# One layer of a hybrid decoder: both output projections with pairs of column blocks and seven products in place of eight

## The chip, the cores and the metric

The kernel runs on one core of a Trainium2 chip. Its engines work from queues of their own: TensorE (PE, matmuls; its weight loads are listed as PEld), VectorE (DVE), ScalarE (ACT), GpSimd (POOL, which here issues DMAs) and SyncE (SP, which issues DMAs). The metric is the time of one execution in microseconds (us) on the device. The kernel before took 1468.19 to 1469.03 us in three runs, with a median of 1468.9 us.

## What is computed

One layer over 256 tokens with a model width of 2048, in float32. Cut to what matters here:

```python
def hybrid_mixer(h, w_in, ...):
    c_q, c_kv, k_r, q_s, k_s, v_s, gates = jnp.split(h @ w_in, offsets, axis=-1)
    ...
    o_a = mla_attention(...)                       # 256 x 2048
    o_b = swa_attention(q_s, k_s, v_s, swa_sinks, rel_table)
    g = jax.nn.sigmoid(gates).reshape(B, S, 2, D_MODEL)
    merged = g[:, :, 0] * (o_a @ w_o_mla) + g[:, :, 1] * (o_b @ w_o_swa)
    return merged @ w_out

def reference(x, ...):
    h = rms_norm(x, norm_mix_pre)
    y = hybrid_mixer(h, ...)
    x = x + rms_norm(y, norm_mix_post)
    h = rms_norm(x, norm_ffn_pre)
    return x + rms_norm(conv_ffn(h, ...), norm_ffn_post)
```

The two products that the change touches are `o_a @ w_o_mla`, called the latent branch's output projection below, and `merged @ w_out`, called the mixer's projection. Each multiplies 256 x 2048 activations by a 2048 x 2048 matrix.

## The kernel before

**How a product is made.** Every float32 product is three matmuls: both operands are split into a high part and a low part, and `mm3` (L175 to L177) adds high by high, high by low and low by high into one PSUM bank. Activations lie transposed in SBUF as sixteen k-rows of 128 x 256 (a high and a low tile each); the 256 tokens are two halves of 128, which are a matmul's stationary operand (128 x 128), and the weights are its moving operand, 512 columns at a time.

**A block.** `gemm` computes 512 columns of the result in eight chunks of two k-rows. For each chunk SP loads 512 KB of weights (`raw`, L131), ACT copies it to the high part (`whi`, L143), DVE subtracts to get the low part (`wlo`, L144), and PE makes 2 k-rows x 2 token halves x 3 = 12 matmuls. The tiles come from rings: RAW = 3 raw tiles and RING = 4 pairs of `whi` and `wlo`, and two "flex" tiles are added to the raw ring or to the other, as `flex[0]` says. So the loads and splits run a few chunks ahead of PE.

**A pair.** `pair_gemm` computes two blocks (1024 columns) in eight units of two k-rows, in the order of a string. A plain unit "p" is 24 matmuls with two SP loads and two splits of 1024 columns. A unit "s" makes seven products of 128 x 128 by 128 x 512 (21 matmuls) from sums of its operands in place of eight. For it `place()` names two tiles, POOL loads the two k-rows into them (L227 the even row, L228 the odd one), DVE makes four sums of 128 x 512 of the weights (L232 to L235, in the tiles of `sums()`), and four splits follow, of the odd row, half of the even row, and the two tiles of sums. `token_sums` (L278 to L284, then a split, L317 and L318) makes the sums of the activations for one unit. The last "s" ends with additions over four more PSUM banks q1, q5, q7, q6 (L255 to L261). The two token halves and two blocks need four banks c11 to c22, so a pair occupies all eight banks. Before the change the branch gates (c and q banks named `cg`, `qg`, order "psppspsp") and the down projection of the FFN (`cd`, `qd`; `cdb`, `qdb`) use it.

**The stretch that is changed.** The gates `ta` of the latent branch are the last work of the input's projection. POOL stores them (L904, `ta_d`). Then the latent branch's projection runs as four single blocks over `wo_a` on the activation tiles `AH` and `AL`; before each block `merge_loads` has POOL load `ta` and the other branch's result `yb` for its 512 columns (tiles `lta`, `lyb`), and after it DVE forms (1 + ta) x acc + yb in `lta` (L955 and L956). A chunk or two into the next block, `m_cols` transposes this on PE (`mT`, L935) and ACT and DVE split it into the slots `mt` (L320, L321), which are the activation of the mixer's projection. That one again runs as four blocks over `w_out` (`flex[0] = "w"` from its start); each is squared and summed on ACT (L972) and multiplied by the norm's gain `gpost` on DVE (L973) into `yg`. The last block feeds the residual sum, the transposes for the FFN (`x2T`), and then the FFN itself.

**What sets the order.** `at(t, f)` puts a function into the step that ends chunk t; `tick()` runs the functions due. A scheduler then sets each engine's order from that of the program: it keeps near it, but puts an instruction behind others whose operands and tiles come free earlier. `late_loads` spreads twelve SP loads over the first block: four of `gpost`, eight of `x` for the residual. Pool `px` holds the `whi` and `wlo` ring tiles and three spare pairs; pool `p6` holds `gpost` (tag "gp") and `yg` (tags "fa" and "fb", two of 128 x 1024 each).

## Time and profile before

| what | value |
|---|---|
| runs | 1468.19 to 1469.03 us, median 1468.9 |
| the profiled execution | 1470.05 us, of which its span is 1468.3 |
| PE busy | 1456.9 us, 7576 instructions |
| DVE busy, ACT busy | 1067.2 us, 830.5 us |
| gates end, latent branch's projection starts | about 553.5 us |
| mixer's projection | about 645 to 735 us |
| granted TensorE clock in these stretches | 1.00 |

The profile is that of one execution: its span is the time from the first to the last instruction, and 1.75 us of the 1470.05 lie outside it. Times in it are microseconds from the span's start. A matmul of 512 columns is listed with some 0.39 us from start to end, but matmuls are pipelined, so what each costs is the distance from one start to the next. In a row of instructions "out<-in" names the tiles, "xN" the count, and what stands in brackets is the idle time before it and what ended that.

### The profile page before, as it was taken

The page shows a single profiled execution, that of the slowest core. Times are in us where ns is not written, and L with a number is a line of the kernel's source. Part 1 is how long each engine was busy: PE and PEld are TensorE (multiplying, and loading weights), DVE is VectorE, ACT ScalarE, POOL GpSimd, SP SyncE. Part 2 cuts the span into 40 slices and gives each one's busy share as a digit, 9 for nine tenths or more (in the row PEclk, how much of TensorE's full clock was granted, in tenths as well). Part 3 has the DMA queues.
Part 4 walks back from the last instruction along what each step waited for, and adds up shares of the span by engine and source line. Part 5 has one row for each costly group of instructions (what it writes and reads, how often), then busy time and mean ns, then how long its engine had stood idle before and what let it go on. Part 6 is the DMA issues. An engine that isn't in the chain of part 4 may idle for free.

```text
span 1468.3 us, 20938 instructions
## 1 busy us (share of the span) xinstructions
PE 1456.9 (99%) x7576; PEld 1244.8 (85%) x7576; DVE 1067.2 (73%) x1881; ACT 830.5 (57%) x1372; POOL 64.9 (4%) x113
## 2 busy tenths in 40 slices
PE   9999999999999999999999999999999999999997
PEld 7888888888888888888888888888888888888886
DVE  7688896745667665555699976778776687677775
ACT  7588874543555554444566655555454565555453
POOL 0011110000000000000000000000000000000000
PEclk9999999999999999999999999999999999999999
DMA  8755376466655559756766666665656666667573
GB/s 297 211 164 167 108 259 192 162 212 200 191 156 160 164 163 334 226 184 212 225 205 185 188 193 193 187 187 187 218 174 213 198 187 189 187 197 233 163 237 129
DMA packets 149909, 287.60 MB, mean 196 GB/s; under 512 B 18428, under 2 KB 29597, under 8 KB 149677
## 3 DMA queue, kind: packets, MB, share of 16 engines
q1 hardware_dynamic: 141312, 256.80, 56.5%
q0 software_dynamic: 8400, 29.41, 6.4%
q8 instruction: 59, 0.97, 0.3%
q14 instruction: 46, 0.37, 0.1%
q10 hardware_dynamic: 92, 0.05, 0.0%
HBM read 277.79 MB, written 8.44 MB: 195 GB/s over the span
## 4 chain that ended last, share of the span: by engine, by line
PE 97%; DVE 2%; ACT 1%; issue 0%; DMA 0%; DVEq 0%; ACTq 0%
PE accg L175 13%; PE accg L177 13%; PE accg L176 13%; PE ub L1147 10%; PE ua L1147 10%; PE ua L1151 5%; PE ub L1151 5%; PE cd L177 2%; PE cd L175 2%; PE cd L176 2%; PE cdb L175 1%; PE cdb L177 1%; PE cdb L176 1%; PE mpo L875 1%; PE cg L176 1%; PE cg L177 1%
## 5 line engine op out<-in xcount | busy, mean ns | idle before, releaser
L144 DVE TENSOR_TENSOR wlo<-raw,whi 128x1024 fp32r<-128x1024 f32 (+2 forms) x476 | 576.3, 1214 | 282.5 <-ACT whi L143 275.2
L143 ACT CAST whi<-raw 128x1024 fp32r<-128x1024 f32 (+2 forms) x476 | 494.7, 1043 | 427.5 <-PE accg L177 172.3
L175 PE MATMUL accg<-whi,ahl 128*128 128x512 f32 (+1 forms) x480 | 187.9, 392 | 0.0
L177 PE MATMUL accg<-whi,ahl 128*128 128x512 f32 (+1 forms) x480 | 185.6, 387 | 0.0
L176 PE MATMUL accg<-wlo,ahl 128*128 128x512 f32 (+1 forms) x480 | 184.8, 385 | 0.0
L1147 PE MATMUL ua<-ahl,whi 128*128 128x512 f32 x640 | 154.6, 391 | 0.0
L1147 PE MATMUL ub<-ahl,whi 128*128 128x512 f32 x640 | 154.6, 391 | 0.0
L175 PE MATMUL accg<-whi,bhl 128*128 128x512 f32 x378 | 148.2, 392 | 0.0
L177 PE MATMUL accg<-whi,bhl 128*128 128x512 f32 x378 | 147.4, 390 | 0.0
L176 PE MATMUL accg<-wlo,bhl 128*128 128x512 f32 x378 | 147.3, 390 | 0.0
L1147 PEld LDWEIGHTS ub<-ahl,whi 128*128 128x128 f32 x640 | 117.5, 188 | 22.9 <-ACT cc L1045 0.2
L1147 PEld LDWEIGHTS ua<-ahl,whi 128*128 128x128 f32 x640 | 117.6, 188 | 22.7
L177 PEld LDWEIGHTS accg<-whi,ahl 128*128 128x128 f32 x480 | 90.1, 188 | 18.0
L176 PEld LDWEIGHTS accg<-wlo,ahl 128*128 128x128 f32 x480 | 90.3, 188 | 15.6
L175 PEld LDWEIGHTS accg<-whi,ahl 128*128 128x128 f32 x480 | 90.3, 188 | 15.5
L1151 PEld LDWEIGHTS ub<-ahl,wlo 128*128 128x128 f32 x640 | 82.2, 191 | 3.2
L1151 PEld LDWEIGHTS ua<-ahl,wlo 128*128 128x128 f32 x640 | 82.2, 191 | 3.1
L1151 PE MATMUL ua<-ahl,wlo 128*128 128x256 f32 x640 | 83.7, 283 | 0.0
L177 PEld LDWEIGHTS accg<-whi,bhl 128*128 128x128 f32 x378 | 71.0, 188 | 14.8
L176 PEld LDWEIGHTS accg<-wlo,bhl 128*128 128x128 f32 x378 | 71.0, 188 | 14.5
L1151 PE MATMUL ub<-ahl,wlo 128*128 128x256 f32 x640 | 83.2, 283 | 0.0
L175 PEld LDWEIGHTS accg<-whi,bhl 128*128 128x128 f32 x378 | 71.0, 188 | 14.3
(545 smaller groups left out, 2218.9 us busy)
## 6 DMA issues: line engine op xcount, KB each, us to landing
raw<-in_ffn_w_up_dram SPq DMA_DIRECT2D x176, 512.0 KB, 4.5
raw<-in_w_in_dram SPq DMA_DIRECT2D x105, 512.0 KB, 4.5
raw<-in_ffn_w_down_dram SPq DMA_DIRECT2D x68, 512.0 KB, 4.5
raw<-in_w_o_swa_dram SPq DMA_DIRECT2D x32, 512.0 KB, 4.4
raw<-in_w_o_mla_dram SPq DMA_DIRECT2D x32, 512.0 KB, 4.5
raw<-in_w_out_dram SPq DMA_DIRECT2D x32, 512.0 KB, 4.1
bias<-strip POOLq DMA_DIRECT2D x16, 256.0 KB, 4.4
raw<-in_mla_w_q_up_dram SPq DMA_DIRECT2D x32, 128.0 KB, 2.8
```

Of the source, the lines that this page charges most:

```text
L143: act.copy(hi[:, a:b], raw[:, a:b])
L144: vec.tensor_tensor(lo[:, a:b], raw[:, a:b], hi[:, a:b].bitcast(F32), op=ALU.subtract)
L175: pe.matmul(o, ah, bh, start=start, stop=False)
L176: pe.matmul(o, ah, bl, start=False, stop=False)
L177: pe.matmul(o, al, bh, start=False, stop=stop)
L875: pe.matmul(o, w(t), p_[:, c], start=n == 0, stop=n == 5)
L1147: pe.matmul(acc[i], hi[:, c], hn[p][:, j * 512:(j + 1) * 512], start=p + j == 0, stop=stop)
L1151: pe.matmul(acc[i][:, 0:256], lo[:, c], hn[p][:, j * 512:j * 512 + 256], start=False, stop=False)
```

## The change

The latent branch's projection becomes a single block 0, a pair of blocks 1 and 2 in the order "pppsppsp" (two units of seven), and a single block 3. The mixer's projection becomes a pair of blocks 0 and 1 in the order "ppspspsp" (three units of seven), and single blocks 2 and 3. Single blocks 0 and 3 of the first and 2 of the second write to the PSUM banks "s", since the pairs take "acc" first.

The sums of tokens for the seven products are made ahead: `a_sums` (tiles `as0`, `as1`) in the course of block 0, `m_sums` (`ms0`, `ms1`) during the first pair, and `ms2` in block 3. The tiles that these and the POOL loads need are all spare ones taken in turn: the spare `whi` and `wlo` tiles of `px` hold `as`, `ms`, the second unit's `ar2hi` and `ar2lo` of the first pair, `lyb2` and the odd units' `mr` of the second pair; the "gp" tile holds `ar1`, the temporary `mtmp` and `mr2` before `gpost`; "fa" and "fb" hold the temporaries `at`, the sums `ta` of the weights and `ud` before `yg`. Therefore `gpost` is now loaded by POOL, two chunks after the second unit of the mixer's pair, in place of SP during block 0. `lta` has four buffers in place of three. The two flex tiles stay with the raw ring until the last block of the mixer's projection. The pool after `es4` opens behind the pair.

```diff
     es6, p6 = open_pool("p6")
-    gpost = sb(p6, [P, D], "gpost", tag="gp")
+    gpost = []
     def late_loads(i):
         if i < 4:
-            nc.sync.dma_start(gpost[:, i * 512:(i + 1) * 512], g_mix_post[i * 512:(i + 1) * 512].partition_broadcast(P))
+            if i == 0:
+                gpost.append(sb(p6, [P, D], "gpost", tag="gp"))
+            pool.dma_start(gpost[0][:, i * 512:(i + 1) * 512], g_mix_post[i * 512:(i + 1) * 512].partition_broadcast(P))
         else:
             t, j = divmod(i - 4, 4)
             nc.sync.dma_start(x2[t][j], x[t * P:(t + 1) * P, j * 512:(j + 1) * 512])
                 pe.transpose(pt[:, i * 256 + t * P:i * 256 + (t + 1) * P], ld[t][0][:, c:c + P], ident)
         split_to(mth[p][:, :], mtl[p][:, :], pt, 0.5)
-    def merge_loads(j):
+    def merge_loads(j, kinds="ab"):
         ld = []
         for t in range(NT):
-            a = sb(p4, [P, 512], f"lta{j}_{t}", tag="lta", bufs=3)
-            b = sb(p4, [P, 512], f"lyb{j}_{t}", tag="lyb", bufs=2)
-            pool.dma_start(a, ta_d[j, t])
-            pool.dma_start(b, yb_d[j, t])
-            ld.append((a, b))
+            both = []
+            for kind, tag, src, bufs in (("a", "lta", ta_d, 4), ("b", "lyb", yb_d, 2)):
+                if kind in kinds:
+                    both.append(sb(p4, [P, 512], f"{tag}{j}_{t}", tag=tag, bufs=bufs))
+                    pool.dma_start(both[-1], src[j, t])
+            ld.append(both)
         return ld
-    for i in range(12):
+    as_ = {}
+    def a_sums(u):
+        st = sb(px, [P, 1024], f"as{u}", F32R, tag="w" + ("hi", "lo")[u % 2])
+        tmp = sb(p6, [P, 1024], f"at{u}", tag="f" + "ab"[u % 2], bufs=2)
+        as_[u] = token_sums(at_[u].bitcast(F32), tmp[:, 0:512], tmp[:, 512:1024], st[:, 0:512], st[:, 512:1024])
+    def merged(a, b, acc):
+        vec.scalar_tensor_tensor(a, a, 1.0, acc, op0=ALU.add, op1=ALU.mult)
+        vec.tensor_tensor(a, a, b, op=ALU.add)
+    a_done = [0]
+    def a_place():
+        a_done[0] += 1
+        i = a_done[0]
+        if i % 2:
+            both = sb(p6, [P, D], f"ar{i}", tag="gp")
+            return both[:, 0:1024], both[:, 1024:2048]
+        return [sb(px, [P, 1024], f"ar{i}{n}", tag="w" + n) for n in ("hi", "lo")]
+    ud_a = []
+    def f_pair(name):
+        return [sb(p6, [P, 1024], f"{name}{n}{cnt[0]}", tag="f" + n, bufs=2) for n in "ab"]
+    def ud_place():
+        ud_a[:] = [x_[:, j * 512:(j + 1) * 512] for x_ in f_pair("ud") for j in range(2)]
+        return ud_a
+    def single(j, lead=3):
+        ld = merge_loads(j)
+        acc, _ = gemm(AH, AL, wo_a, 0, KT, 512 * j, 512, ps=(pss, "s"))
+        for t in range(NT):
+            merged(*ld[t], acc[t])
+        for p in range(2):
+            at(now[0] + lead + p, lambda p=2 * j + p, ld=ld: m_cols(p, ld))
+    def a_pair():
+        lds = [merge_loads(1), merge_loads(2, "a")]
+        both = sb(px, [P, 1024], "lyb2", tag="whi")
+        for t in range(NT):
+            lds[1][t].append(both[:, t * 512:(t + 1) * 512])
+            pool.dma_start(lds[1][t][1], yb_d[2, t])
+        c = pair_gemm("a", wo_a, 0, 512, A_ORDER, lambda k, t: (AH(k)[:, t * P:(t + 1) * P], AL(k)[:, t * P:(t + 1) * P]),
+                      lambda u: as_[u], 0, ud_place, a_place, lambda: f_pair("ta"))
+        def pair_evac(i):
+            t, j = divmod(i, 2)
+            vec.tensor_tensor(ud_a[i], ud_a[i], c[i], op=ALU.add)
+            merged(*lds[j][t], ud_a[i])
+        for n_, i in enumerate((0, 2, 1, 3)):
+            at(now[0] + n_, lambda i=i: pair_evac(i))
+        for p in range(2, 6):
+            at(now[0] + 2 + p, lambda p=p: m_cols(p, lds[p // 2 - 1]))
+    for u in range(A_ORDER.count("s")):
+        at(now[0] + 1 + 3 * u, lambda u=u: a_sums(u))
+    for i in range(4, 12):
         at(now[0] + 10 + 2 * i, lambda i=i: late_loads(i))
-    for j in range(4):
-        ld = merge_loads(j)
-        acc, _ = gemm(AH, AL, wo_a, 0, KT, 512 * j, 512)
-        for t in range(NT):
-            a, b = ld[t]
-            vec.scalar_tensor_tensor(a, a, 1.0, acc[t], op0=ALU.add, op1=ALU.mult)
-            vec.tensor_tensor(a, a, b, op=ALU.add)
-        for p in range(2):
-            at(now[0] + (3 if j == 3 else 1) + p, lambda p=2 * j + p, ld=ld: m_cols(p, ld))
+    ms = {}
+    def m_sums(u):
+        st = sb(px, [P, 1024], f"ms{u}", F32R, tag="w" + ("hi", "lo")[u % 2])
+        tmp = sb(p6, [P, D], f"mtmp{u}", tag="gp")
+        ms[u] = token_sums(mt[u].bitcast(F32), tmp[:, 0:512], tmp[:, 512:1024], st[:, 0:512], st[:, 512:1024])
+    single(0)
+    for u, t in ((0, 9), (1, 12)):
+        at(now[0] + t, lambda u=u: m_sums(u))
+    a_pair()
     yg_all = [[sb(p6, [P, 1024], f"yg_{t}_{j}", tag="f" + "ab"[t], bufs=2) for j in range(2)] for t in range(NT)]
     yg = [[yg_all[t][j // 2][:, (j % 2) * 512:(j % 2 + 1) * 512] for j in range(4)] for t in range(NT)]
+    at(now[0] + 6, lambda: m_sums(2))
+    single(3, 2)
     blocks = [(0, 512), (512, 512), (1024, 512), (1536, 256), (1792, 256)]
     NB = len(blocks)
     W_BLOCKS = [(512 * j, 512) for j in range(4)]
...
-        vec.tensor_tensor(yg[t][j][:, o:o + n], acc[t][:, :n], gpost[:, c0:c0 + n], op=ALU.mult)
+        vec.tensor_tensor(yg[t][j][:, o:o + n], acc[t][:, :n], gpost[0][:, c0:c0 + n], op=ALU.mult)
...
-    flex[0] = "w"
-    turn.update(raw=0, w=0)
-    for b in range(4):
+    w_done = [0]
+    def w_place():
+        w_done[0] += 1
+        i = w_done[0]
+        if i % 2:
+            return [sb(px, [P, 1024], f"mr{i}{n}", tag="w" + n) for n in ("hi", "lo")]
+        both = sb(p6, [P, D], f"mr{i}", tag="gp")
+        at(now[0] + 2, *(lambda k=k: late_loads(k) for k in range(4)))
+        return both[:, 0:1024], both[:, 1024:2048]
+    def w_pair():
+        d = [yg[t][j] for t in range(NT) for j in range(2)]
+        c = pair_gemm("w", w_out, 0, 0, W_ORDER, lambda k, t: (MH_(k)[:, t * P:(t + 1) * P], ML_(k)[:, t * P:(t + 1) * P]),
+                      lambda u: ms[u], 0, d, w_place, lambda: [yg_all[t][1] for t in range(NT)])
+        def pair_evac(i):
+            t, j = divmod(i, 2)
+            vec.tensor_tensor(d[i], d[i], c[i], op=ALU.add)
+            act.activation(jk(f"yj{j}_{t}"), d[i], AF.Square, accum_out=ssy[t][:, j:j + 1])
+            vec.tensor_tensor(d[i], d[i], gpost[0][:, j * 512:(j + 1) * 512], op=ALU.mult)
+        for i in range(4):
+            at(now[0] + i, lambda i=i: pair_evac(i))
+    w_pair()
+    es4.close()
+    es8, p8 = open_pool("p8")
+    for b in range(2, 4):
         c0, n = W_BLOCKS[b]
         last = b == 3
-        acc, todo = gemm(MH_, ML_, w_out, 0, KT, c0, n, split=0 if last else None, extra={i: (px,) for i in range(EXTRA)} if last else None)
-        if b == 0:
+        if last:
+            flex[0] = "w"
+            turn.update(raw=0, w=0)
+        acc, todo = gemm(MH_, ML_, w_out, 0, KT, c0, n, split=0 if last else None, extra={i: (px,) for i in range(EXTRA)} if last else None,
+                         ps=None if last else (pss, "s"))
+        if last:
             drain()
-            es4.close()
-            es8, p8 = open_pool("p8")
-        if last:
             y_evac(acc, b, 0)
             resid(0)
             finish_tile(acc[1], todo)
...
+A_ORDER = "pppsppsp"
+W_ORDER = "ppspspsp"
```

The program has 15 matmul rows fewer on PE (7386 rows before, 7371 now). The instructions move as follows at three places.

**DVE during block 0 of the latent branch's projection.** `wlo` are the splits of the block's chunks, four of which precede these rows; `at` is the temporary of the token sums, `bhl` the activation's slots. Before:

```order
L144 TENSOR_TENSOR wlo_5912<-raw_5909,whi_5911 128x1024
L144 TENSOR_TENSOR wlo_5930<-raw_5927,whi_5929 128x1024
L144 TENSOR_TENSOR wlo_5948<-raw_5945,whi_5947 128x1024
L144 TENSOR_TENSOR wlo_5966<-raw_5963,whi_5965 128x1024
L144 TENSOR_TENSOR wlo_5984<-raw_5981,whi_5983 128x1024
L144 TENSOR_TENSOR wlo_6002<-raw_5999,whi_6001 128x1024
```

Now:

```order
L144 TENSOR_TENSOR wlo_5938<-raw_5935,whi_5937 128x1024
L278 TENSOR_TENSOR at_5909<-bhl_4096 128x512
L144 TENSOR_TENSOR wlo_5956<-raw_5953,whi_5955 128x1024
L281 TENSOR_TENSOR at_5909<-at_5909 128x128
L282 TENSOR_TENSOR at_5909<-at_5909 128x128
L283 TENSOR_TENSOR at_5909<-at_5909 128x128
L278 TENSOR_TENSOR at_5972<-bhl_4097 128x512
L284 TENSOR_TENSOR at_5909<-at_5909 128x128
L281 TENSOR_TENSOR at_5972<-at_5972 128x128
L282 TENSOR_TENSOR at_5972<-at_5972 128x128
L283 TENSOR_TENSOR at_5972<-at_5972 128x128
L144 TENSOR_TENSOR wlo_5983<-raw_5980,whi_5982 128x1024
```

The sums of two units stand between the splits of the chunks, up to eight rows of them between one split and the next.

**POOL from the stores of the last gates on.** Each row is a DMA that POOL issues; in brackets are the counters that it waits for (DMASW the queue's own earlier DMAs, then PE, ACT and DVE). `ta_0_5832` and `ta_1_5835` are the last gates. Before:

```order
L904 DMA ta_d<-ta_0_5832 128x512 [waits DMASW2_49,Activation_49]
L904 DMA ta_d<-ta_1_5835 128x512 [waits DMASW3_49,Activation_49]
L944 DMA lyb_0_6022<-yb_d 128x512 [waits DMASW6_49,DMASW4_49,DVE_49]
L944 DMA lyb_1_6026<-yb_d 128x512 [waits DMASW5_49,DMASW0_49,DVE_49]
L943 DMA lta_1_6025<-ta_d 128x512 [waits PE_49]
L943 DMA lta_0_6196<-ta_d 128x512 [waits DMASW7_49,PE_49]
L944 DMA lyb_0_6197<-yb_d 128x512 [waits DMASW4_49,DVE_49]
```

Now:

```order
L904 DMA ta_d<-ta_0_5832 128x512 [waits DMASW3_49,Activation_49]
L904 DMA ta_d<-ta_1_5835 128x512 [waits DMASW4_49,Activation_49]
L227 DMA ar_6179<-in_w_o_mla_dram 128x1024 [waits DMASW5_49,DMASW4_49,DMASW3_49]
L228 DMA ar_6179<-in_w_o_mla_dram 128x1024 [waits DMASW6_49]
L994 DMA lyb_6050<-yb_d 128x512 [waits DMASW7_49]
L994 DMA lyb_6050<-yb_d 128x512 [waits DMASW0_49]
L228 DMA ar2lo<-in_w_o_mla_dram 128x1024 [waits DMASW1_49]
L947 DMA lyb_0_6040<-yb_d 128x512 [waits DMASW2_49,DVE_49]
L947 DMA lyb_1_6044<-yb_d 128x512 [waits DVE_49]
L947 DMA lta_0_6046<-ta_d 128x512 [waits PE_49]
L947 DMA lta_1_6048<-ta_d 128x512 [waits DMASW5_49,PE_49]
L227 DMA ar2hi<-in_w_o_mla_dram 128x1024 [waits DMASW6_49,PE_49,Activation_49]
```

Four loads of weight rows of 512 KB (`ar` twice, `ar2lo`, `ar2hi`) stand in this queue now, among the loads for the merge; `ar2hi`, the last, waits for PE and ACT as well.

**DVE at the start of the mixer's projection.** `lta` are the merged columns of the latent branch's last block, `mT` the transposes, `ahl` their slots. Before:

```order
L955 SCALAR_TENSOR_TENSOR lta_0_6372<-lta_0_6372,accg_0_6380 128x512
L955 SCALAR_TENSOR_TENSOR lta_1_6376<-lta_1_6376,accg_1_6381 128x512
L956 TENSOR_TENSOR lta_0_6372<-lta_0_6372,lyb_0_6373 128x512
L956 TENSOR_TENSOR lta_1_6376<-lta_1_6376,lyb_1_6377 128x512
L144 TENSOR_TENSOR wlo_6624<-raw_6621,whi_6623 128x1024
L144 TENSOR_TENSOR wlo_6649<-raw_6646,whi_6648 128x1024
L144 TENSOR_TENSOR wlo_6674<-raw_6671,whi_6673 128x1024
L144 TENSOR_TENSOR wlo_6692<-raw_6689,whi_6691 128x1024
L144 TENSOR_TENSOR wlo_6710<-raw_6707,whi_6709 128x1024
L144 TENSOR_TENSOR wlo_6740<-raw_6737,whi_6739 128x1024
L321 SCALAR_TENSOR_TENSOR ahl_5849<-mT_6639,ahl_5849 128x512
L144 TENSOR_TENSOR wlo_6758<-raw_6755,whi_6757 128x1024
```

Now:

```order
L144 TENSOR_TENSOR wlo_6708<-raw_6705,whi_6707 128x1024
L144 TENSOR_TENSOR wlo_6735<-mr1lo,whi_6734 128x1024
L232 TENSOR_TENSOR yg_1_6413<-mr1hi 128x512
L233 TENSOR_TENSOR yg_1_6413<-mr1lo,mr1hi 128x512
L234 TENSOR_TENSOR yg_1_6415<-mr1lo,yg_1_6413 128x512
L144 TENSOR_TENSOR wlo_6753<-mr1hi,whi_6752 128x512
L235 TENSOR_TENSOR yg_1_6415<-mr1lo,yg_1_6415 128x512
L144 TENSOR_TENSOR wlo_6760<-yg_1_6413,whi_6759 128x1024
L321 SCALAR_TENSOR_TENSOR ahl_5849<-mT_6698,ahl_5849 128x512
L232 TENSOR_TENSOR yg_1_6413<-mr_6815 128x512
L233 TENSOR_TENSOR yg_1_6413<-mr_6815 128x512
L144 TENSOR_TENSOR wlo_6770<-yg_1_6415,whi_6769 128x1024
```

The splits of plain chunks, which followed each other, now have the weights' sums (L232 to L235), the split of half a row (128x512) and the splits of `yg` between them, and the slots `ahl` behind several of these.

## The prediction

> **What bounds the kernel now.** I read the page first, then the windows over the two projections, then single timelines.
>
> ```profile
> span 1468.3 us, 20938 instructions
> ...
> PE 1456.9 (99%) x7576; PEld 1244.8 (85%) x7576; DVE 1067.2 (73%) x1881; ACT 830.5 (57%) x1372; POOL 64.9 (4%) x113
> ...
> PE 97%; DVE 2%; ACT 1%; issue 0%; DMA 0%; DVEq 0%; ACTq 0%
> ```
>
> PE is busy for 99% of the span, and the chain of waits followed back from the end stays on PE for 97% of it. So a matmul left out shortens the end, as long as what feeds PE keeps up. In the windows (columns: span of the window, then PE, PEld, DVE, ACT, POOL, granted clock, DMA share, GB/s) the first row is the gates' pair, the other two are the projections that change:
>
> ```profile
> 242.60:284.70 42.10, 42.10 (x186) 34.34 (x185) 29.41 (x32) 21.91 (x23) 2.17 (x4) 1.00 0.44 149
> 553.50:645.00 91.50, 91.50 (x417) 75.68 (x416) 51.64 (x54) 39.02 (x42) 6.99 (x13) 1.00 0.75 253
> 645.00:735.00 90.00, 89.82 (x408) 74.01 (x407) 55.14 (x69) 45.85 (x69) 2.18 (x4) 1.00 0.67 216
> ```
>
> PE is never idle in the first projection and for 0.18 us in the second (the tail to the FFN, which is not changed); the clock is full. DVE works for 51.64 + 55.14 = 106.8 of 181.5 us, ACT for 84.9. The slack for the change's extra work is there on average; whether it is there at the right moments is the question.
>
> **What a matmul costs.** Ends are modelled, so starts count:
>
> ```profile
> 574.66 0.39 PE L176 MATMUL accg<-wlo,bhl 128*128 128x512 f32 x1
> ...
> 580.10 0.39 PE L176 MATMUL accg<-wlo,bhl 128*128 128x512 f32 x1
> ```
>
> 24 starts lie between them: 5.44 / 24 = 0.2267 us. The five units of seven make 21 matmuls in place of 24, so **15 x 0.2267 = 3.40 us** leave PE. Transposes, chunks and the tail keep their number. The Trainium skill ("TensorE: Matmul & The Clock Gate", section "Wait — 56ns, not 53.3ns?") gives N / 2.4 GHz + about 2.5 ns from start to start, 215.7 ns at 512 columns; by it the 15 would be worth 3.24 us. This trace has 226.7 ns for the very matmuls, and that decides.
>
> Do the new products run as fast? Their stationary operands are sums (`as`, `ms`) in other tiles. The trace has two such cases, with 0.389 us and about 0.395 us a piece, and the latter's spacing:
>
> ```profile
> L175 PE MATMUL qd<-whi,s x21: 389/389/389, 1011.6 to 1112.3; 128*128 128x512 f32 x21
> ```
> ```profile
> L177 PE MATMUL qg<-whi,xs x9: 390/395/404, 250.7 to 278.3; 128*128 128x512 f32 x9
> ```
> ```profile
> 264.76 0.40 PE L175 MATMUL cg<-whi,xs 128*128 128x512 f32 x1
> ...
> 268.02 0.40 PE L177 MATMUL qg<-whi,xs 128*128 128x512 f32 x1
> ```
>
> The second is 3.26 / 14 = 0.2329 us a start, 0.006 more. With some 15 such matmuls a seven that is 0.1 us a seven at most, 0.5 us for five. I take nothing, since the down projection's `s` is the same use, and keep 0.5 as the bound. A gain beyond 3.40 I exclude: no PE wait is there to be removed.
>
> **What the sevens cost the other engines.** DVE's distances back to back, from the gates' pair:
>
> ```profile
> 279.63 0.68 DVE L256 TENSOR_TENSOR tb<-tb,qg 128x512 f32<-128x512 f32 x1
> 280.23 1.22 DVE L144 TENSOR_TENSOR wlo<-raw,whi 128x1024 fp32r<-128x1024 f32 x1
> 281.36 0.68 DVE L257 TENSOR_TENSOR tb<-tb,qg 128x512 f32<-128x512 f32 x1
> 281.96 1.22 DVE L144 TENSOR_TENSOR wlo<-raw,whi 128x1024 fp32r<-128x1024 f32 x1
> ```
>
> A split takes 1.13 us, a 512-wide operation 0.60. A seven needs three splits, half a split and four sums: 3 x 1.13 + 5 x 0.60 = 6.4 us of DVE for 21 x 0.2267 = 4.76 us of PE, so alone it falls behind; a plain unit needs 2.27 for 5.44. One of each is 8.7 of 10.2 us: DVE catches up only in the plain units. ACT, at 1.055 us a split (next fence), needs 3.8 us a seven. The token sums, from those of the gates' pair:
>
> ```profile
> L143 ACT CAST whi<-raw 128x1024 fp32r<-128x1024 f32 x68 | 71.3, 1055 | 91.0 <-PE accg L177 65.1 <-DMA raw<-in_w_out_dram 18.4 <-PE accg L176 3.7
> ```
> ```profile
> L278 DVE TENSOR_TENSOR xa<-ahl 128x512 f32<-128x512 f32 x3 | 2.0, 679 | 0.0
> ...
> L281 DVE TENSOR_TENSOR xm<-xa 128x128 f32<-128x128 f32 x3 | 0.8, 277 | 0.0
> ```
>
> A unit's are 0.60 + 4 x 0.28 + 0.60 = 2.3 us. In all DVE gets 5 x (6.4 - 2.27) + 5 x 2.3 + 8 x 0.60 (the additions over the q banks) + 8 x 0.60 (the pairs' evictions into SBUF) = 42 us, and comes to 149 of 178 us, 84%; ACT gets some 12 and comes to 97. All of it lies beside PE if each split ends before its chunk is due. The nearest precedent is the down projection, with seven units of seven:
>
> ```profile
> 1004.20:1130.00 125.80, 125.80 (x557) 104.20 (x556) 97.93 (x114) 64.11 (x73) 6.33 (x12) 1.00 0.59 196
> ```
>
> DVE at 78% there, and 125.80 / 0.2267 = 555 starts (two more records are cut by the window's edges): no loss at all. The gates' pair lost one split's lateness in three sevens:
>
> ```profile
> its engine sat idle before it (us, times) until:
>   DVE wlo L144: 0.3, 1
> ```
>
> So the cost of a seven is between 0 and 0.3 us of PE, up to 1.5 us for five. I take 0, since I can follow the three tight places by the clock:
>
> **First place, block 0.** DVE's first token sum uses memory of the old gates, so it waits until POOL's last stores have landed. SP's first `gpost` load waits for the same in the run before:
>
> ```profile
> 553.85 1.23 POOL L904 DMA_DIRECT2D ta_d<-ta  x2 [2.86 <-ACT ta L903]
> ```
> ```profile
> 553.21 3.62 SPq L131 DMA_DIRECT2D raw<-in_w_o_mla_dram  x2
> 559.88 0.34 SPq L922 DMA_DIRECT2D gpost<-in_norm_mix_post_dram  x1
> ```
>
> So 559.9. Behind that sum the splits of chunks 4 to 7 are queued on DVE, and PE waits for those. Block 0 starts at 553.3, a chunk is 12 x 0.2267 = 2.72 us, so they are due at 564.2, 566.9, 569.6, 572.4. By the operations queued they end at 561.6 (0.60 + 1.13), 565.3 (2.6 of sums, 1.13), 567.9 and 570.3: the least margin is 1.6 us. Ahead of chunk 6's split stands a sum (L232) that needs the even row of the first unit, a POOL load issued at about 559.9 too. In its queue:
>
> ```profile
> rr<-in_ffn_w_down_dram POOLq DMA_DIRECT2D x8, 512.0 KB, 5.2
> ...
> gr<-in_w_in_dram POOLq DMA_DIRECT2D x6, 512.0 KB, 5.4
> ```
>
> Landing takes 5.4 us at the median, and may take 8.0: then the sum starts at 567.9, and with 0.60 + 1.13 the split ends at 569.6, as it is due.
>
> **Second place, the first pair.** `ar2hi` is issued only when the first seven's sixth product has let its tile go, 18 starts or 4.1 us into that unit; behind it in POOL's queue nothing is due soon. Two plain units follow, then the second seven, whose fourth product (the first that needs a sum of the weights) is due at 4.76 + 10.88 + 9 starts = 17.7 us. From the landing on DVE has five operations of 512 columns and two splits to do, 5.3 us, so the row may land at 12.4, 8.3 us after its issue, at no cost. DVE's tightest split there has 0.9 us, the start of single block 3 about 1 us.
>
> **Third place, start of the mixer's pair (E).** The last merge's `lta` loads wait for transposes that end at E - 6.2; `mr1hi` behind them lands by about E + 1 and is needed at E + 8.7 (two plain units less the 2.2 us of its splits). The splits here, behind the slots and sums of the diff's third piece, end 0.6 to 1.6 us early: the least margin of all. `gpost` goes out once the second seven's rows are split, at about E + 19.4; with four issues at the 0.61 us of `ta_d` (1.23 for two) and the slowest landing quoted below, 7.7, it is there by E + 29.6, against a use at the pair's end, E + 42 (5 x 5.44 + 3 x 4.76 us): it costs nothing, and without the rest of the pair as cover its landing would. The ring of `whi` and `wlo` with four pairs in place of six until the last block also costs nothing: the first projection ran with four and never idled.
>
> **The sum.** Span 1468.3 - 3.40 = 1464.9; the profiled execution 1470.05 - 3.40 = 1466.65. That execution was 1.15 us above the median of the runs, so a median of 1468.9 - 3.40 = **1465.5 us**.
>
> **Rivals.** *DVE is late in the sevens* (17%). For it: 84% of DVE against 78% in the down projection (97.93 of 125.80), margins of 0.6 us at the third place, the gates' 0.3 us. Against: the down projection's zero with 7 sevens in 24 units; the mixer's pair, with 3 in 8, is the denser one. At 0.3 us each, 1.5 us: 1467.0; at twice that 1468.5. *The new products run at the slower spacing* (10%): 1465.5 + 0.5 = 1466.0. *POOL's loads of weight rows land late* (10%), the case on the other side. In the window 571 to 574 us the DMA engines are full (share 1.05):
>
> ```profile
> 571.00:574.00 3.00, 3.00 (x15) 2.46 (x14) 1.51 (x2) 1.05 (x1) 0.00 (x0) 1.00 1.05 393
> ```
> ```profile
> DMA to landing us min/median/max: 4.0/5.4/7.7
> ```
>
> and the slowest of the `gr` loads, in this second fence, took 7.7 us, close to the 8.0 and 8.3 that are free. Each us beyond costs one at each place: at twice the median, 10.8 us, 2.8 + 2.5 = 5.3 us, 1470.8; from 11.4 us on (3.4 + 3.1 = 6.5: 1472.0) it decides, at 12 it is 1473.2. Against it: 1 MB of `gpost` leaves just that stretch. The Trainium skill ("SBUF — State Buffer", section "🔬 SBUF: two separate sides") would make such lateness a matter of DVE: it says that the descriptors of a DMA issued from POOL cannot be written while a DVE operation holds a port pair that the two share, so that the DMA seems blocked. By it a busy DVE would hold these loads back. The `gr` loads ran beside a DVE with 29.41 of 42.10 us busy and still landed in 5.4 us, so the trace does not show it. That the change doesn't do what it says is excluded: 15 rows are gone. Other ways have 3%.
>
> **How the numbers follow.** The forecast has 60%. The measurement can tell 0.2%, 2.9 us, from nothing: faster is below 1466.0, slower above 1471.8. Faster is the forecast and the half of the second rival that stays below its bound, less a little for noise: 0.63. The first rival, the rest of the second and the mild half of the third make 0.25, slower 0.12. The range goes from the fastest run shown less 3.40, 1464.8, to the first rival at its dearest, 1468.5, which leaves out the POOL rival and the rest.
>
> **What would show it.** PE rows 15 fewer, starts still 0.2267 apart in both pairs, no idle time of PE that ended with `wlo` or a DMA: right. PE idle before a product of block 0's chunk 6 or of a seven, ended by DVE, says first rival, or third if DVE itself waited for `ar`, `ar2hi` or `mr` loads; spacing of 0.233 on products with `as` and `ms` says the second. The forecast is wrong if the two projections take more than 178.6 us together (181.5 - 3.4, and half a microsecond).

## The result, and the profile after

The changed kernel took 1466.89 us at the median of 22 runs (1465.6 to 1468.28), the kernel before 1468.9 (1467.86 to 1470.05, 22 runs). The ratio is 0.9986 with a 95% interval of 0.9981 to 0.9992: faster by 1.2 to 2.8 us. That is clear of no change, but on the near side of the 0.2% that the prediction called faster.

The page of the changed kernel:

```profile
span 1463.8 us, 20998 instructions
...
PE 1452.9 (99%) x7561; PEld 1240.7 (85%) x7561; DVE 1104.9 (75%) x1957; ACT 841.8 (58%) x1389; POOL 72.4 (5%) x127
...
PE 93%; issue 3%; DVE 2%; DMA 1%; ACT 1%; POOL 0%; DVEq 0%; ACTq 0%; POOLq 0%
```

PE has 15 instructions fewer, as it should. But the chain that ended last, 97% PE before, now leaves PE for 7% of the span. Among the longest pieces of that chain outside PE are these (start, length, what):

```profile
588.73 6.13 issue
594.88 8.25 DMA ar2hi<-in_w_o_mla_dram
...
1343.59 14.33 issue
```

The last lies in the down projection of the FFN, which the change does not touch; PE stood still there for 0.2 us (`cdb` in the next rows), and not at all when the same kernel was profiled again (after_again). The first two are the prediction's second place: the load of the even weight row of the latent pair's second seven. The waits of PE show what it cost (total, times, longest), in us:

```profile
PE warm L77 <- DVE ramp L66: 1.1, 1, 1.1
PE qa L176 <- DVE wlo L144: 0.7, 2, 0.6
PE pstrip L349 <- DMA sel<-in_strip_sel_dram: 0.3, 1, 0.3
PE cdb L176 <- DVE wlo L144: 0.2, 1, 0.2
```

The first and third belong to the start of the kernel; the second is new; the fourth is the one in the down projection. The start of the kernel differs from one execution to the next: the last attention product before the projections (`mpo`) came at 547.70 us in the profile before and at 545.38 in this one, 2.3 us apart, in code that the change does not touch; in the other runs below it lies between 544.8 and 546.3. So what follows is measured on a stretch inside one execution: **from the start of the last `mpo` matmul to the start of the first `x2T` transpose**, which holds both projections. It is 179.12 us before (547.70 to 726.82) and 176.99 us after (545.38 to 722.38): 2.13 us less, where 15 x 0.2267 = 3.40 were forecast. Of the forecast, 1.27 us are missing.

### The profile page after: what moved, and what is told of

Same layout as the page of the kernel before. It is cut to its first block, busy times and chain, and to the rows that moved or that the text cites. A ratio compares the mean times of both kernels' runs of the same rounds, so it can differ in the third digit from the quotient of the medians.

```text
span 1463.8 us, 20998 instructions
## 1 busy us (share of the span) xinstructions
PE 1452.9 (99%) x7561; PEld 1240.7 (85%) x7561; DVE 1104.9 (75%) x1957; ACT 841.8 (58%) x1389; POOL 72.4 (5%) x127
## 4 chain that ended last, share of the span: by engine, by line
PE 93%; issue 3%; DVE 2%; DMA 1%; ACT 1%; POOL 0%; DVEq 0%; ACTq 0%; POOLq 0%
PE accg L175 11%; PE accg L177 11%; PE accg L176 11%; PE ua L1240 10%; PE ub L1240 9%; PE ua L1244 5%; PE ub L1244 5%; PE cd L176 2%; PE cd L175 2%; PE cd L177 2%; PE mpo L875 1%; PE cw L177 1%; PE cg L175 1%; PE cg L177 1%; PE cw L176 1%
## 5 line engine op out<-in xcount | busy, mean ns | idle before, releaser
L144 DVE TENSOR_TENSOR wlo<-raw,whi 128x1024 fp32r<-128x1024 f32 (+2 forms) x466 | 562.5, 1213 | 219.1 <-ACT whi L143 212.6
L143 ACT CAST whi<-raw 128x1024 fp32r<-128x1024 f32 (+2 forms) x466 | 483.3, 1042 | 375.2 <-PE accg L177 125.8
L175 PE MATMUL accg<-whi,ahl 128*128 128x512 f32 (+1 forms) x416 | 162.9, 392 | 0.0
L177 PE MATMUL accg<-whi,ahl 128*128 128x512 f32 (+1 forms) x416 | 160.7, 386 | 0.0
L176 PE MATMUL accg<-wlo,ahl 128*128 128x512 f32 (+1 forms) x416 | 159.9, 384 | 0.0
L175 PE MATMUL accg<-whi,bhl 128*128 128x512 f32 x314 | 123.0, 392 | 0.0
L177 PE MATMUL accg<-whi,bhl 128*128 128x512 f32 x314 | 122.5, 390 | 0.0
L176 PE MATMUL accg<-wlo,bhl 128*128 128x512 f32 x314 | 122.4, 390 | 0.0
L177 PEld LDWEIGHTS accg<-whi,ahl 128*128 128x128 f32 x416 | 78.1, 188 | 15.5
L176 PEld LDWEIGHTS accg<-wlo,ahl 128*128 128x128 f32 x416 | 78.2, 188 | 13.2
L175 PEld LDWEIGHTS accg<-whi,ahl 128*128 128x128 f32 x416 | 78.2, 188 | 13.0
L177 PEld LDWEIGHTS accg<-whi,bhl 128*128 128x128 f32 x314 | 58.9, 188 | 12.2
L175 PEld LDWEIGHTS accg<-whi,bhl 128*128 128x128 f32 x314 | 59.0, 188 | 12.0
L176 PEld LDWEIGHTS accg<-wlo,bhl 128*128 128x128 f32 x314 | 59.0, 188 | 12.0
```

Of the source, the lines that this page charges most:

```text
L143: act.copy(hi[:, a:b], raw[:, a:b])
L144: vec.tensor_tensor(lo[:, a:b], raw[:, a:b], hi[:, a:b].bitcast(F32), op=ALU.subtract)
L175: pe.matmul(o, ah, bh, start=start, stop=False)
L176: pe.matmul(o, ah, bl, start=False, stop=False)
L177: pe.matmul(o, al, bh, start=False, stop=stop)
```

## The experiments

All times of stretches are from one profiled execution each. "Without loss" is 179.12 less 0.2267 us for each matmul left out.

| kernel | matmuls fewer | stretch | without loss | lost | median of runs, of before beside it | ratio, 95% interval |
|---|---|---|---|---|---|---|
| the change | 15 | 176.99 | 175.72 | 1.27 | 1466.89, 1468.9 | 0.9986 [0.9981, 0.9992] |
| the change again (after_again) | 15 | 177.24 | 175.72 | 1.52 | 1466.21, 1468.06 | 0.9987 [0.9978, 0.9996] |
| load_early | 15 | 176.79 | 175.72 | 1.07 | 1465.1, 1468.6 | 0.9978 [0.9968, 0.9987] |
| load_early_pin | 15 | 175.67 | 175.72 | -0.05 | 1464.45, 1468.3 | 0.9974 [0.9964, 0.9984] |
| the same again (pin_again) | 15 | 175.67 | 175.72 | -0.05 | 1464.71, 1468.06 | 0.9977 [0.9968, 0.9986] |
| late_ms13 | 15 | 180.08 | 175.72 | 4.36 | 1469.71, 1468.6 | 1.001 [1.0, 1.0019] |
| ms_13_pin | 15 | 175.67 | 175.72 | -0.05 | 1464.56, 1468.3 | 0.9973 [0.9962, 0.9984] |
| order_early | 15 | 175.76 | 175.72 | 0.04 | 1464.99, 1468.3 | 0.9975 [0.9965, 0.9985] |
| order_close | 15 | 179.86 | 175.72 | 4.14 | 1468.58 (one run), 1468.3 | - |
| w_only | 9 | 177.03 | 177.08 | -0.05 | 1466.41, 1468.6 | 0.9986 [0.9976, 0.9996] |
| a_only | 6 | 179.46 | 177.76 | 1.70 | 1468.41, 1468.6 | 1.0005 [0.9996, 1.0015] |

The intervals of the ratios reach 0.8 to 1.6 us to either side, as much as most of what is to be told apart, so each verdict below goes by the stretch. The two kernels that were profiled twice repeat it within 0.25 us (the change) and 0.01 us (load_early_pin); the kernel before was profiled once.

**What the trace of the change shows at the wait.** PE's timeline (start, length, engine, line, operation, in brackets the idle time and what ended it), in the second seven:

```profile
606.86 0.39 PE L177 MATMUL ca<-whi,as 128*128 128x512 f32 x1
607.09 0.39 PE L175 MATMUL qa<-whi,bhl 128*128 128x512 f32 x1
608.05 0.50 PE L176 MATMUL qa<-wlo,bhl 128*128 128x512 f32 x1 [0.57 <-DVE wlo L144]
608.38 0.39 PE L177 MATMUL qa<-whi,bhl 128*128 128x512 f32 x1
608.61 0.40 PE L175 MATMUL qa<-whi,as 128*128 128x512 f32 x1
609.18 0.50 PE L176 MATMUL qa<-wlo,as 128*128 128x512 f32 x1 [0.17 <-DVE wlo L144]
```

Between 607.09 and 608.05 lie 0.96 us in place of 0.23, and 0.57 between 608.61 and 609.18: 0.73 + 0.34 = 1.07 us. The start right behind each is 0.1 late as well (608.05 to 608.38), which makes the 1.27. The first wait is that of the seven's third product, for the split of half the even row (`wlo<-ar2hi` below), the second that of its fourth, for the split of the weights' sums (`wlo<-taa`). Both are DVE's. DVE's own timeline shows that DVE was late because it stood still:

```profile
592.89 4.63 DVE L144 TENSOR_TENSOR wlo<-raw,whi 128x1024 fp32r<-128x1024 f32 x4
...
603.15 0.69 DVE L232 TENSOR_TENSOR taa<-ar2hi 128x512 f32<-128x512 f32 x1 [5.11 <-DMA ar2hi<-in_w_o_mla_dram]
...
606.10 0.68 DVE L318 TENSOR_TENSOR ms<-mtmp,ms 128x512 fp32r<-128x512 f32 x1
...
607.31 0.68 DVE L144 TENSOR_TENSOR wlo<-ar2hi,whi 128x512 fp32r<-128x512 f32 x1
607.91 1.22 DVE L144 TENSOR_TENSOR wlo<-taa,whi 128x1024 fp32r<-128x1024 f32 x1
```

5.11 us idle before the first reader of `ar2hi`, then everything in a row: a late load, not a full DVE. Two theories were set against each other all the same, since PE's wait names DVE: **the late load**, and **DVE too full** in the pair.

**Does it recur?**

> The changed kernel itself, beside the version that cured its wait. If the two waits of PE in the latent pair's second seven belong to the kernel and not to one execution, they stand in this profile too: the stretch from the last attention product to the first x2T is 176.9 to 177.2 us and ar2hi lands 8 us after its issue. Otherwise it is 175.7 to 176.5 us.

It does: 177.24 us, two waits of PE for `qa`, `ar2hi` landed 8.5 us after its issue (8.2 in the first profile). 0.3 us later there, 0.25 us more lost.

**The load earlier.**

```diff
-        both = sb(px, [P, 1024], "lyb2", tag="whi")
+        both = sb(px, [P, 1024], "lyb2", tag="wlo")
```

> The changed kernel with one tile renamed: the second block's yb shares the spare wlo tiles instead of the whi ones, so that ar2hi finds a free tile and its load no longer waits for the first seven's sixth product. Measure: from the last attention product (mpo) to the first x2T transpose, 179.12 us before and 176.99 us in the changed kernel, where PE stood still twice in the second seven of the latent branch. Theory (the load of ar2hi is late because it is issued late and then shares the DMA engines with four weight loads of SP): PE's two waits vanish and the stretch is 179.12 - 3.40 = 175.7 us, the time 1465.5 or a little below. Rival (DVE is too full in the first pair, the load only comes last by chance): DVE's work is the same, so the waits stay at 0.5 us or more and the stretch is 176.2 to 177.0 us.

Neither came as a whole: the waits in the second seven are gone, as the theory said, but the stretch, 176.79, lies in the rival's range. A new one stands in the plain unit ahead, and it is the same load again. DVE's timeline of load_early:

```profile
594.12 0.69 DVE L232 TENSOR_TENSOR taa<-ar2hi 128x512 f32<-128x512 f32 x1 [1.38 <-DMA ar2hi<-in_w_o_mla_dram]
594.73 4.63 DVE L144 TENSOR_TENSOR wlo<-raw,whi 128x1024 fp32r<-128x1024 f32 x4
```

With the load issued 6 us earlier, the scheduler put its first reader ahead of the four splits of plain rows; the row came 5.4 us after its issue, and DVE held four splits back for 1.38 us, the first of which had all it needed (ACT's copies of three of them begin at 591.66 and take about 1 us each). PE then waited for the first of them (0.80 us, at 596.00).

**The load earlier, and its readers behind those splits.** In addition to the line above:

```diff
-            vec.tensor_tensor(ta[:, lo_], even[:, hi_], even[:, lo_], op=ALU.subtract)
-            vec.tensor_tensor(ta[:, hi_], odd[:, hi_], even[:, hi_], op=ALU.subtract)
+            (tc.keep_in_program_order if name == "a" and last else id)(vec.tensor_tensor(ta[:, lo_], even[:, hi_], even[:, lo_], op=ALU.subtract))
+            (tc.keep_in_program_order if name == "a" and last else id)(vec.tensor_tensor(ta[:, hi_], odd[:, hi_], even[:, hi_], op=ALU.subtract))
```

> load_early with one thing more: in the latent pair's second seven the two sums that read ar2hi (L232, L233) are pinned behind DVE's split of ar2lo, so that DVE's queue holds the four splits of the plain rows ahead of them, as in the changed kernel. DVE's rows are then those of the changed kernel; only ar2hi is issued some 6 us earlier. Theory (the load lands late, and DVE stands before its first reader with ready splits queued behind): no wait of PE is left in the pair, the stretch from the last attention product to the first x2T is 175.7 us, the time about 2 us below the one of load_early's before less 3.4: 1465.0 to 1465.5 us. Rival (DVE too full in the pair): the same DVE work is there, so 0.5 to 1.3 us of PE waits stay, 176.2 to 177.0 us.

175.67 us: all of the 3.40 us, and no wait of PE in either pair. DVE's timeline of load_early_pin:

```profile
593.50 4.62 DVE L144 TENSOR_TENSOR wlo<-raw,whi 128x1024 fp32r<-128x1024 f32 x4
...
600.60 0.69 DVE L232 TENSOR_TENSOR taa<-ar2hi 128x512 f32<-128x512 f32 x1
```

The same DVE work lies in the pair as in the changed kernel, with `ar2hi` issued at 589.33 and read at 600.60. The theory of a full DVE falls here. The order on DVE is not quite that of the changed kernel, as the expectation had it: the split of `ar2lo` now stands ahead of these sums, and the mixer's L318 behind the split of `ar2hi`, as it does in load_early too. The new order with the load still late was not run, so what the order alone is worth was not tried. Beside the changed kernel on one chip:

> load_early_pin on the same chip as the changed kernel. Theory: its stretch is 175.7 us again, 1.3 us below that of the changed kernel, and the medians differ by 1 to 1.7 us. Rival (the gain of load_early_pin over the changed kernel was the chip of that day): the medians agree within 0.5 us.

175.67 again; 1464.71 against 1466.21 us, 1.50 us less, and 3.35 less than the kernel before: the 3.40 us of the forecast.

**The sums moved.** The other way to relieve DVE is to take the mixer's token sums out of the pair's middle, once with the load late and once with it early. late_ms13:

```diff
-        both = sb(px, [P, 1024], "lyb2", tag="whi")
...
-            lds[1][t].append(both[:, t * 512:(t + 1) * 512])
+            lds[1][t].append(sb(px, [P, 1024], f"lyb2{t}", tag="whi")[:, 0:512])
...
-    for u, t in ((0, 9), (1, 12)):
+    for u, t in ((0, 13), (1, 14)):
```

> The changed kernel with the mixer's token sums ms0 and ms1 moved out of the first pair's middle (steps 9 and 12) to its end (13 and 14), and ar2hi made to wait for the same tile as in the changed kernel, by giving the second block's yb two spare whi tiles. Theory (late load): ar2hi is still issued after the first seven's sixth product, lands 7 to 8 us later, and PE still waits; the stretch stays at 176.5 to 177.1 us. Rival (DVE too full): the sums no longer stand ahead of the splits, the waits vanish, 175.7 us.

ms_13_pin has the last of these three edits and the two pinned sums of load_early_pin:

> The mixer's sums moved to steps 13 and 14 as in late_ms13, but ar2hi in a free tile, so that it loads with the first seven's rows some 35 us earlier, and its readers pinned as in load_early_pin. Theory (the late load made late_ms13 slow, its sums only added to DVE's backlog behind it): no wait of PE, 175.7 us. Rival (the sums in the second seven by themselves make DVE late): 0.4 to 3 us of waits stay, 176.1 to 178.7 us.

180.08 us with the load late, 3.1 us worse than the change, which neither theory expected; 175.67 with it early, nothing lost. So the sums at this place cost nothing by themselves; behind a late load they do. DVE's and then ACT's timeline of late_ms13:

```profile
603.38 0.69 DVE L232 TENSOR_TENSOR taa<-ar2hi 128x512 f32<-128x512 f32 x1 [5.65 <-DMA ar2hi<-in_w_o_mla_dram]
...
607.06 0.69 DVE L144 TENSOR_TENSOR wlo<-ar2hi,whi 128x512 fp32r<-128x512 f32 x1
608.43 0.69 DVE L318 TENSOR_TENSOR ms<-mtmp,ms 128x512 fp32r<-128x512 f32 x1 [0.69 <-ACT ms L317]
609.16 0.69 DVE L278 TENSOR_TENSOR mtmp<-ahl 128x512 f32<-128x512 f32 x1
...
610.09 1.22 DVE L144 TENSOR_TENSOR wlo<-taa,whi 128x1024 fp32r<-128x1024 f32 x1
```
```profile
607.78 0.62 ACT L317 CAST ms<-mtmp 128x512 fp32r<-128x512 f32 x1 [3.70 <-DVE wlo L144]
608.30 1.04 ACT L143 CAST whi<-taa 128x1024 fp32r<-128x1024 f32 x1
```

After 5.65 us of standing still, the split of the weights' sums, for which PE waits, has the mixer's sums ahead of it in two queues: on ACT its high part (`whi`, 608.30) stood behind L317, which by the profile waited 3.70 us, until DVE's split of `ar2hi` (607.06) was done, and on DVE its low part (`wlo`, 610.09) behind L318 and L278. So here the mixer's sums waited for the late row themselves and handed the wait on.

**More and less room between the sevens.** order_early, and order_close behind it:

```diff
-A_ORDER = "pppsppsp"
+A_ORDER = "ppspppsp"
...
-A_ORDER = "pppsppsp"
+A_ORDER = "pppspspp"
```

> The changed kernel with the order ppspppsp in place of pppsppsp in the latent pair: three plain units between the sevens, ar2hi still waits for the first seven. It may land 5.4 us later than before without a loss. Theory: it lands 8 to 9 us after its issue, PE does not wait for it, 175.7 to 176.0 us. Rival (DVE too full in the sevens): a wait of 0.3 us or more in the second seven, 176.0 us or more.

175.76 us, no wait in either pair; `ar2hi` landed 6.8 us after its issue, where 8 to 9 were expected.

> The changed kernel with the order pppspspp: one plain unit between the sevens of the latent pair. The wait for ar2hi is made larger. Theory: issued some 5 us after the first seven begins, landing 5.4 to 8.2 us later, with 5.3 us of DVE behind it, while its product is due 12.2 us after the first seven began: 3.4 to 6.0 us more are lost than without a late load, the stretch is 179.1 to 181.7 us. Rival (DVE too full): one plain unit less to catch up in costs DVE some 3 us of slack, a loss of 1.3 to 2.5 us, 177.0 to 178.2 us.

179.86 us, 4.14 lost, within the theory's range, but not all by the wait. The load landed 6.5 us after its issue, DVE stood before L232 for 3.17 us, and PE's three waits come to 2.0 us. Some 0.9 us of the loss is a fall of the clock behind them, which the last section shows. The other 3.2 us belong to the load: a little less than the theory's 3.4, and more than the 1.3 to 2.5 of its rival.

**One pair alone.** w_only has four single blocks in the latent branch's projection, and of the mixer's pair all:

```diff
-    single(0)
...
-    a_pair()
+    for j in range(3):
+        if j == 2:
+            for u, t in ((0, 2), (1, 5)):
+                at(now[0] + t, lambda u=u: m_sums(u))
+        single(j, 1)
```

> Only the mixer's pair: the latent branch's projection is four single blocks again, the mixer's keeps its three sevens (9 matmuls fewer than before instead of 15). Theory: all of it is gained, the stretch is 179.12 - 9 x 0.2267 = 177.08 us, and no wait of PE stands in the mixer's pair. Rival (DVE late at the start of the mixer's pair): 0.3 us a seven or more lost, 177.4 to 178.0 us.

177.03 us, nothing lost: the densest pair, three sevens of eight units, costs PE no wait. a_only has the latent pair, and the mixer's projection as before, with `gpost` loaded in the latent branch's last block:

```diff
-    for u, t in ((0, 9), (1, 12)):
-        at(now[0] + t, lambda u=u: m_sums(u))
     a_pair()
...
-    at(now[0] + 6, lambda: m_sums(2))
-    single(3, 2)
+    for i in range(4):
+        at(now[0] + 4 + i, lambda i=i: late_loads(i))
+    single(3, 3)
...
-    w_pair()
...
-    for b in range(2, 4):
+    for b in range(4):
```

> Only the latent branch's pair: the mixer's projection is four single blocks as before (6 matmuls fewer than before). As no ms0 is made, ar2hi finds a free tile and loads early. Theory (late load): no wait, the stretch is 179.12 - 6 x 0.2267 = 177.76 us. Rival (DVE too full in the pair, with the sums of ms gone only in part): a wait of 0.3 us or more, 178.1 us or more. Rival (pairs cost something of their own, such as the start of single block 3): 178.0 us or more without a wait that ends with a split.

179.46 us: the six matmuls are not gained but 0.34 us lost. The load was issued early, as the theory had it, and yet it is the load. DVE's timeline of a_only:

```profile
573.04 0.69 DVE L232 TENSOR_TENSOR taa<-ar2hi 128x512 f32<-128x512 f32 x1 [2.19 <-DMA ar2hi<-in_w_o_mla_dram]
...
574.25 1.22 DVE L144 TENSOR_TENSOR wlo<-raw,whi 128x1024 fp32r<-128x1024 f32 x1
```

Here `ar2hi` goes out with the first seven's rows and lands 10.9 us after its issue; its first reader was placed ahead of the split of the pair's first row, and PE waited 1.41 us for that split, in the pair's first products. Here as in load_early, an early load without the pin moved its reader up, and the wait with it.

**Why the load is late** was read from the trace and not tried by itself. POOL's and SP's issues, and the landing of `ar2hi`:

```profile
594.88 0.53 POOL L227 DMA_DIRECT2D ar2hi<-in_w_o_mla_dram  x1 [6.15 <-ACT whi L143]
```
```profile
594.14 0.33 SPq L151 DMA_DIRECT2D raw<-in_w_o_mla_dram  x1
595.27 2.64 SPq L131 DMA_DIRECT2D raw<-in_w_o_mla_dram  x3
```
```profile
DMA to landing us min/median/max: 8.2/8.2/8.2
```

The row names a copy of ACT as what POOL waited for last. But in order_early no copy of ACT ends near the issue (593.27), and it comes 0.95 us after the start of the last matmul that reads the tile (592.32); here it is 0.94 us (593.94 to 594.88). So it is PE's sixth product that lets the load go, as the prediction had it. DVE's four splits in a row (592.89) set four raw tiles free in short order, and SP issued four loads of 512 KB beside it. In the window 601 to 602 us the queues share the DMA engines like this (packets, MB, share; q1 is SP's, q0 POOL's):

```profile
q1 hardware_dynamic: 170, 0.33, 86.2%
q0 software_dynamic: 12, 0.05, 15.1%
```

The load of `mr3hi`, as large, ran from 648.94 us with no packet of SP's until 652.8, and landed in 3.9 us. That a busy DVE holds such loads back, the other thought of the prediction, does not show: POOL's queue had 57% of the engines from 597 to 598, where DVE was busy, and 15% from 601 to 602, where DVE stood still.

## Why the prediction was right or wrong

- **A matmul's worth, 15 x 0.2267 = 3.40 us:** right. Three kernels that lose nothing in the pairs have 175.67 to 175.76 us against 175.72.
- **Slower spacing of the new products (second rival):** wrong. The products with `as` and `ms` take 0.389 us a piece at the median, and run at 0.227 us; in the first seven of the latent pair nine starts in a row, six of them with `as`, lie 0.226 apart (590.77 to 592.58). Only the first ones with `ms` are slower, and they stand behind the transposes at 652.33 (0.24 from 653.46 to 653.70), where the older products are slower too; the later ones at 655.08, 655.31, 655.53 are not:

```profile
653.46 0.40 PE L175 MATMUL cw<-whi,ms 128*128 128x512 f32 x1
653.70 0.39 PE L176 MATMUL cw<-wlo,ms 128*128 128x512 f32 x1
...
655.08 0.39 PE L176 MATMUL qw<-wlo,ms 128*128 128x512 f32 x1
655.31 0.39 PE L177 MATMUL qw<-whi,ms 128*128 128x512 f32 x1
655.53 0.39 PE L175 MATMUL qw<-whi,ms 128*128 128x512 f32 x1
```

  The 0.233 of the gates' pair, from which the rival was made, is something else. In the kernel before it begins with the first product of `xs`, in all three of its sevens, and no transpose or wait stands ahead of it:

```profile
264.30 0.39 PE L176 MATMUL cg<-wlo,ahl 128*128 128x512 f32 x1
264.52 0.40 PE L177 MATMUL cg<-whi,ahl 128*128 128x512 f32 x1
264.76 0.40 PE L175 MATMUL cg<-whi,xs 128*128 128x512 f32 x1
```

  Why it is so there, and not with `s`, `as` and `ms`, stays open.

- **DVE's and ACT's load, 42 and some 12 us more:** 1104.9 - 1067.2 = 37.7 and 841.8 - 830.5 = 11.3 over the whole span. DVE was never the bound: load_early_pin has the same work and no wait. The first rival gave 1.5 us of loss, near the 1.27 measured, for a cause that the runs rule out: the size was right by accident.
- **First place, block 0:** right in the outcome: PE has no wait there. But the landing of 5.4 us was too short here already: the two rows of `ar` took 6.9 and 8.9 us, and DVE stood 1.25 us before its first sum of the weights. The even row's 6.9 us were within the 8.0 that were free.
- **Second place:** here the prediction failed. It said that `ar2hi` "may land at 12.4, 8.3 us after its issue, at no cost", and took 5.4 us for the landing. By that count a landing of 8.2 us would still have been free; but three terms were off. The issue came at 594.88, 0.7 us behind the eighteen starts that were counted (the last of them is at 593.94, the next matmul at 594.17): nothing was allowed for the product's end and the way to POOL. The landing took 8.2 us, 2.8 more: the median of the gates' loads comes from a quieter time (a DMA share of 0.44 in the prediction's window, 0.87 from 594.9 to 603.1 here). And one more operation stood in DVE's queue behind the row, the mixer's L318 at 606.10, 0.60 us. Together 4.1 us, against a margin of 8.3 - 5.4 = 2.9: 1.2 us of the 1.27. The count also dated only the fourth product; PE stood still first at the third, which needs the split of half of that row, and 0.73 us of the 1.27 were lost there. It was the third rival's mechanism, at one place of its two and far below the 11.4 us from which the prediction let it decide.
- **Third place, the mixer's pair:** right. No wait, `gpost` issued at 660.99, 20.2 us after the pair's start at 640.83, where 19.4 was said; `mr1hi` landed at 643.3, 2.5 us after that start, where 1 was said, still well ahead of its use; w_only gains all of its nine matmuls.
- **The time:** 1465.5 was said, 1466.89 came, inside the range of 1464.8 to 1468.5; the 1.39 us between are the wait (1.27 and 1.52 in two profiles). The chance of 0.63 was on faster by over 0.2%; it came out at 0.14%. By its own sign the forecast of no loss is wrong: it allowed the two projections 178.6 us in place of 181.5, and 2.13 us less than 181.5 are 179.4.

## What to carry to other kernels

The margin of a load that is issued only when a tile comes free has three terms: the issue, which came 0.7 us behind the last matmul counted, the landing at a crowded moment (8.2 us here beside four loads of another queue, 3.9 us without them), and every operation that stands between the landing and its use in its engine's queue (0.60 us here). Where its first reader shares a queue with ready work, loading earlier is half of the cure: the reader must also stay behind that work, as load_early (1.07 us lost) and load_early_pin (nothing lost) show. An edit of 1.3 us is seen in the start times of one stretch long before it is seen in run times that spread over 2.7 us (1465.6 to 1468.28).

## What the runs showed of the hardware that was not expected

The clock fell in order_close, in the middle of the kernel. Windows of order_close (span, PE, PEld, DVE, ACT, POOL, granted clock, DMA share, GB/s):

```profile
601.80:604.40 2.60, 0.94 (x3) 0.21 (x2) 2.50 (x5) 1.66 (x2) 0.00 (x0) 1.00 0.02 7
604.40:606.70 2.30, 2.00 (x4) 1.15 (x5) 2.25 (x3) 1.59 (x2) 0.53 (x1) 0.56 0.00 0
606.70:608.20 1.50, 1.50 (x5) 1.13 (x4) 1.50 (x2) 1.50 (x3) 0.00 (x0) 0.54 0.77 216
```

After 2.6 us in which PE was busy for 0.94, the granted clock was 0.56 and 0.54 for some 3.7 us; matmuls started 0.42 us apart (604.45, 604.87, 605.29). PE's timeline of order_close, and DVE's:

```profile
605.29 0.63 PE L175 MATMUL qa<-whi,as 128*128 128x512 f32 x1
606.18 0.79 PE L176 MATMUL qa<-wlo,as 128*128 128x512 f32 x1 [0.26 <-DVE wlo L144]
...
608.31 0.40 PE L175 MATMUL qa<-whi,as 128*128 128x512 f32 x1
```
```profile
604.91 1.22 DVE L144 TENSOR_TENSOR wlo<-taa,whi 128x1024 fp32r<-128x1024 f32 x1
```

Not all of that is loss. The matmul at 606.18 had to wait for the split that ended at 606.13, up to which DVE had no pause since the load landed, so the slow starts ahead of it cost nothing. From there to 608.31 five starts took 2.13 us in place of 1.13; 0.1 us of that follows the other waits too, so the clock cost some 0.9 us beyond the wait. In late_ms13 PE was busy for only 1.66 of 4 us (608 to 612), and the clock stayed at 1.00. The Trainium skill ("TensorE: Matmul & The Clock Gate", section "What's actually happening") tells of a window of 3413 ns that runs free of the kernel's start, and lets the clock fall after an idle window of about that length. The slow part here, some 3.6 us (604.45 to 608.05), is about as long; but PE's longest idle time ahead of it was 1.31 us, so a stretch in which PE was busy in part was enough. No run here moved one wait against such a window, so why the clock held in late_ms13 stays open.

Behind a transpose or a wait the matmuls start a little further apart for a while: in the changed kernel ten starts behind the transposes at 649.12 lie 0.231 us apart (649.79 to 652.10), and six behind the wait at 609.18 lie 0.232 apart (609.52 to 610.91), in place of 0.227. Eight groups of transposes stand in the stretch before the change and after it, so this cancels here.
